# A two-layer hybrid encoder on one core: rope transfers as a task of their own, other planner delays, the fourth head's inputs at another place, decays from still masks in fp32r

## The chip, the core and the metric

The kernel runs on one core of a Trainium2 chip. Its time is the device time of one execution in microseconds, given as the median of three runs. The engines are TensorE (PE: matmuls; PEld: its weight loads), VectorE (DVE), ScalarE (ACT), GpSimd (POOL) and SyncE (SP), which here only issues DMAs. Matmul results go to PSUM accumulators; everything else lies in SBUF.

## The reference

512 tokens (two groups of 256) pass two layers. Each layer has three branches, which share one input projection, and then a convolutional feed-forward part:

```
h = rmsnorm(x) * (1 + sc1) + sh1
p = h @ w_in                                  # one projection, columns split
o_mla = latent attention (low-rank kv, 8 heads, rotary part of width 32)
o_rg  = bidirectional RG-LRU scan
o_gdn = gdn(q, k, v, g_f, beta_f) + flip(gdn(flip(q, k, v, g_b, beta_b)))
m = sum_b sigmoid(gate_b) * (o_b @ w_branch[b]);  x = x + gt1 * (m @ w_out)
x = x + gt2 * ConvGLU(rmsnorm(x) * (1 + sc2) + sh2)
```

`gdn`, the gated delta rule, works in chunks of 64 tokens for each of four heads. The parts that the change touches:

```
g      = cumsum(g within the chunk)
decay  = exp(g_i - g_j)  for j <= i, else 0
A      = strict lower part of (beta k k^T) * decay
Tinv   = (I + A)^-1                           # triangular, per chunk
u, w   = Tinv @ (v beta),  Tinv @ (k beta exp(g))
attn   = (q k^T) * decay;  q_dec = q exp(g);  k_dec = k exp(g_last - g)
per chunk:  v_new = u - w @ state;  o = q_dec @ state + attn @ v_new
            state = state * exp(g_last) + k_dec^T @ v_new
```

## The kernel before

Activations lie with channels on the 128 partitions and the 512 tokens along the free axis. A weight matrix is read in pieces of 128x1024 (tile `raw`, four buffers, issued by SP at L378). ACT rounds each piece to fp32r (`wh`, L391) and DVE takes the rest (`wl`, L298, the helper `sub`). Activations are split in the same way (`hh`, `hl`), and a product is three fp32r matmuls of 128x512 (`mm3`, recorded at L220 like every matmul, since all pass the class `Tensor`).

**The order.** The queues of TensorE and SP follow the order in which the program emits their instructions; those of DVE, ACT and POOL are put in order by a scheduler. The program emits with a planner of its own. The string `BRANCHES` (L33) lists the jobs of a layer's branches: `in6` the first projections; `uq.j`, `uk.j` the queries and keys of attention; `gq.h`, `gk.h`, `gv.h` a GDN head's inputs; `x`, `g`, `b` those of the RG-LRU; `z` the output gate of GDN; `gate.b.d` and `br.b.d` the gate and the projection of branch b; `close` and `mid` sums. Jobs are emitted in that order as fast as a counted clock (`Driver.now`, in planner us, raised by each matmul) goes on. Beside them run generators, the tasks: each emits some instructions and then yields a number from `SLACK` (L61), the planner us after which it goes on. A number so says how much matmul work of the jobs is emitted between one step of a task and the next. `drv.until(event)` holds the jobs until an event's time: the clock jumps from one task's due time to the next, and those tasks' steps are emitted there.

**Rope.** `query(j)` (from L793) computes the attention queries; for j = 5 DVE has the rotated halves ready, and SP sends them to DRAM and back into `Qt` (`drope`, L812; `Qt`, L814):

```
dr = dp.tile([P, 2, T], F32, name="drope", tag="drope")
nc.sync.dma_start(dr, x)
for e in range(2):
    nc.sync.dma_start(Qt[64 + 16 * e:80 + 16 * e], dr.rearrange(...)[e])
ev_q.set(SLACK["rope"])
```

The three DMAs are emitted at once, and the attention's first step waits on `ev_q`.

**Decays.** `solve(h)` (from L1339) handles a GDN head, both directions d and four pairs of chunks t. DVE multiplies the strict mask by the column of g (`gw`, L1355: 128x512 for a direction); TensorE multiplies each 128x128 block of it by the mask `inc` (`gdn_z`, four fp32 matmuls for a direction), and ACT takes the exponential (`E`). A third `gw` (L1373, two halves of 128x256, g against ones) makes `gdn_eg`, from which ACT and DVE make `qd`, the decayed q. `gw` has two buffers, `E` four.

**The inverse.** `gdn_gram`, in two groups, multiplies k by k and by q; DVE forms `B` from it. SP sends the diagonal blocks (`cb`, L1408) to DRAM and back as `Lb`; POOL substitutes in 15 steps (`xt`, `X`, L292 and L298); SP sends the result to DRAM (`dx`, L1440, eight DMAs) and back as `W` (L1444 and L1445, four DMAs). Then `combine` (from L1452) multiplies `W` and `B` on TensorE (`gdn_l16`, `gdn_l32`, `gdn_l64`; a view that joins them prints `gdn_l`). The delays between these steps are `ws`, `z`, `gw`, `eg`, `gram`, `cb`, `dl`, `X`, `dx`, `W`. A head's scan follows: `gdn_rec` (the state), `gdn_o` (the output), and for its norm `ssq` and `spread`.

The constants (masks, identity, ones, selectors) lie in one fp32 tile `cs`, read by one DMA at the start.

Of the kernel before, what the change touches and what calls it, by code (L numbers as in the profile page):

```python
# [8 lines left out]
F32 = mybir.dt.float32  # L9
F32R = mybir.dt.float32r  # L10
# [3 lines left out]
ALU = mybir.AluOpType  # L14
# [4 lines left out]
P = 128  # L19
T = 512  # L20
S = 256
# [15 lines left out]
    g.2 x.3 b.2.0 gate.1.2 b.2.1 gq.2 gk.2 gv.2 gate.1.3 g.3 b.3.0 gate.1.4 b.3.1 gate.1.5 gate.1.6  # L37
    br.1.0 br.1.1 gq.3 br.1.2 z.0 gk.3 br.1.3 gate.2.0 gv.3 gate.2.1 br.1.4 z.1 gate.2.2 br.1.5
    gate.1.7 z.2 br.1.6 gate.2.3 gate.2.4 br.1.7 gate.2.5 z.3 gate.2.6 mid gate.2.7 br.2.0 br.2.1
    br.2.2 br.2.3 br.2.4 br.2.5 br.2.6 br.2.7"""  # L40


def jobs():
# [17 lines left out]
SLACK = {  # L61
    "modev": 0.7, "att_s": 3.2, "att_t": 1.8, "att_e": 1.0, "low_rank": 11.8, "low_rank_out": 152.5, "mla": 0.2,
# [172 lines left out]
def _body(es, tc, nc, xT, cT, wall, wmod, pvec, fng, cst, rope, xinit, yT, dbg):  # L235
    V, A, G = nc.vector, nc.scalar, nc.gpsimd
    drv = Driver()
    PE = Tensor(nc.tensor, drv)
    depth = pvec.shape[1]

    cp = es.enter_context(tc.tile_pool(name="const", bufs=1))
    sp = es.enter_context(tc.tile_pool(name="small", bufs=1))
# [5 lines left out]
    dp = es.enter_context(tc.tile_pool(name="dr", bufs=2, space=DRAM))  # L248
# [19 lines left out]
    ident, ones = C("ident"), C("ones")  # L268
# [4 lines left out]
    dx = [[dp.tile([8, P, 32], F32, name=f"dx{i}{j}", tag=f"dx{i}{j}", bufs=1) for j in range(2)] for i in range(2)]  # L273
# [391 lines left out]
    for k in range(8):  # L665
        t = xp.tile([P, T], F32, name="x", tag="x")
# [8 lines left out]
    for k in range(8):  # L675
        t = stp.tile([P, T], F32, name="sq", tag="t", bufs=4)
# [11 lines left out]
    r = aux_tile(name="spread")  # L688
# [19 lines left out]
    for l in range(depth):  # L708
# [84 lines left out]
        def query(j):  # L793
            if j == 0:
                drv.until(ev_cq)
            ps = gemm(cq)
            if j < 4:
                A.activation(Qt[0:64, 2 * j, :], ps[0:64], AF.Copy, scale=96.0 ** -0.5)
                A.activation(Qt[0:64, 2 * j + 1, :], ps[64:128], AF.Copy, scale=96.0 ** -0.5)
                return  # L800
            cosq, sinq = rep2(rt_[:, 0, :]), rep2(rt_[:, 1, :])
            if j == 4:
                lr["rope"] = mp.tile([P, 4, T], F32, name="rope", tag="Vt")
            ab = lr["rope"][:, 2 * j - 8:2 * j - 6, :]
# [12 lines left out]
        def values():
            Vt = lr["Vt"] = mp.tile([P, 4, T], F32, name="Vt", tag="Vt")
# [250 lines left out]
        for job in JOBS:  # L1069
# [92 lines left out]
            elif k == "out":  # L1162
                d, g = ix
# [23 lines left out]
            elif k == "down":  # L1187
                d, g = ix
# [7 lines left out]
                t = x1[d]  # L1196
# [10 lines left out]
                if (d, g) == (7, 0):  # L1207
                    h = {}
# [16 lines left out]
class GDN:  # L1225
# [16 lines left out]
    def gates(self, ab):  # L1242
        V, A, G, PE = self.V, self.A, self.G, self.PE
        sp, C = self.sp, self.C
# [4 lines left out]
        al = sp.tile([P, 4, 8], F32, name="al_", tag="al_")  # L1249
# [89 lines left out]
    def solve(self, h):  # L1339
# [395 lines left out]
```

## Time and profile before

| | |
|---|---|
| median of three runs | 2016.12 us (2014.07 to 2019.35) |
| the profiled execution | 2019.3 us |
| its span in the trace | 2017.5 us |
| mean granted TensorE clock | 0.986 of full speed |
| PE / DVE / ACT / POOL busy | 1949.8 / 1235.5 / 823.9 / 258.0 us |
| PE instructions; bytes moved by DMA | 11563; 231.44 MB |

An engine's waits are printed as what the idle time before an instruction ended with, in total, number and longest. The timeline gives each record's start and duration; matmul records overlap, so the time that one costs is read from the start of the next. The granted clock (PEclk) is 1 for full speed. Line L220 stands for every matmul, so the tiles' names tell them apart.

### The profile page before, as it was taken

What the parts mean: (1) busy time and instruction counts of PE and PEld (TensorE: products, weight loads), DVE (VectorE), ACT (ScalarE), POOL (GpSimd) and SP (SyncE); (2) the same over time, 40 slices, a digit from 0 to 9 for tenths busy, and PEclk for the clock granted to TensorE, in tenths of its full rate; (3) what the DMA queues carried; (4) which work ended last, traced back from release to release, by engine and by line L of the source; (5) the groups of instructions that cost most, each with busy time, mean ns of one, the idle gap of its engine ahead of it and who ended that gap; (6) DMA issues with size and microseconds to landing.
All of it is one profiled execution on the core that took longest, in us unless ns stands there. A gap on an engine that the chain in (4) does not pass through costs nothing.

```text
span 2017.5 us, 29521 instructions
## 1 busy us (share of the span) xinstructions
PE 1949.8 (97%) x11563; PEld 1564.2 (78%) x11563; DVE 1235.5 (61%) x2324; ACT 823.9 (41%) x1275; POOL 258.0 (13%) x511
## 2 busy tenths in 40 slices
PE   9999999989999999999999999999898999999998
PEld 5777777768777888887877777777687888888887
DVE  5765776755456766652357758776553677676534
ACT  3444366523323544432234534655222344444322
POOL 1100162132200100000011004513130010000000
PEclk9999999999999999999999999999999999999999
DMA  8131443443325233353533123443432533333233
GB/s 318 63 115 53 111 129 113 122 129 94 92 97 186 95 94 104 95 178 106 192 121 94 63 74 113 120 141 110 124 76 74 214 100 94 96 96 100 94 97 102
DMA packets 141851, 231.44 MB, mean 115 GB/s; under 512 B 79760, under 2 KB 84240, under 8 KB 141712
## 3 DMA queue, kind: packets, MB, share of 16 engines
q1 hardware_dynamic: 136240, 221.95, 35.4%
q10 hardware_dynamic: 5472, 7.61, 1.1%
q8 instruction: 91, 1.49, 0.3%
q14 instruction: 48, 0.39, 0.1%
HBM read 221.66 MB, written 7.86 MB: 114 GB/s over the span
## 4 chain that ended last, share of the span: by engine, by line
PE 82%; DVE 5%; POOL 4%; DMA 4%; issue 2%; ACT 2%; SPq 2%; POOLq 0%; ACTq 0%; DVEq 0%
PE mm_up L220 24%; PE mm_down L220 12%; PE mm_gate L220 10%; PE mm_br L220 6%; PE mm_in L220 3%; PE mm_out L220 3%; PE mm_gk L220 2%; PE mod L220 2%; PE mm_gq L220 2%; POOL xt L292 2%; PE mm_gv L220 2%; POOL X L298 2%; PE att_s L220 1%; PE gdn_rec L220 1%; PE gdn_l L220 1%
## 5 line engine op out<-in xcount | busy, mean ns | idle before, releaser
L298 DVE TENSOR_TENSOR wl<-raw,wh 128x1024 fp32r<-128x1024 f32 x304 | 374.0, 1232 | 322.2 <-ACT wh L391 321.6
L391 ACT CAST wh<-raw 128x1024 fp32r<-128x1024 f32 x304 | 318.3, 1049 | 485.3 <-PE mm_down L220 127.9
L220 PE MATMUL mm_up<-hh,wh 128*128 128x512 f32 x704 | 275.8, 392 | 3.4 <-POOL hh L308 3.4
L220 PE MATMUL mm_up<-hl,wh 128*128 128x512 f32 x704 | 275.3, 391 | 0.0
L220 PE MATMUL mm_up<-hh,wl 128*128 128x512 f32 x704 | 275.1, 391 | 0.0
L301 DVE SCALAR_TENSOR_TENSOR cv<-mm_up,pv,cv 128x510 f32<-128x510 f32 x176 | 131.2, 748 | 61.3 <-ACT cv L571 58.0
L220 PE MATMUL mm_gate<-hh,wh 128*128 128x512 f32 x384 | 163.8, 427 | 0.3
L220 PEld LDWEIGHTS mm_up<-hh,wh 128*128 128x128 f32 x704 | 133.0, 189 | 31.6 <-POOL hh L308 3.9
L220 PEld LDWEIGHTS mm_up<-hl,wh 128*128 128x128 f32 x704 | 133.0, 189 | 28.0 <-DVE hl L298 0.3
L220 PEld LDWEIGHTS mm_up<-hh,wl 128*128 128x128 f32 x704 | 133.0, 189 | 27.6
L220 PE MATMUL mm_gate<-hl,wh 128*128 128x512 f32 x384 | 151.2, 394 | 0.0
L220 PE MATMUL mm_gate<-hh,wl 128*128 128x512 f32 x384 | 151.0, 393 | 0.0
L220 PE MATMUL mm_down<-ah,wh 128*128 128x512 f32 (+1 forms) x396 | 145.9, 369 | 0.0
L220 PE MATMUL mm_down<-ah,wl 128*128 128x512 f32 (+1 forms) x396 | 144.9, 366 | 0.6 <-DVE wl L298 0.6
L220 PE MATMUL mm_down<-al,wh 128*128 128x512 f32 (+1 forms) x396 | 144.7, 365 | 0.0
L308 POOL TENSOR_SCALAR hh<-hn 128x256 fp32r<-128x256 f32 x64 | 34.4, 549 | 663.8 <-ACT hn L588 661.2
L571 ACT ACTIVATE cv<-mm_up,pv 128x512 f32<-128x512 f32 x88 | 68.5, 780 | 88.9 <-PE mm_up L220 88.9
L220 PEld LDWEIGHTS mm_gate<-hh,wh 128*128 128x128 f32 x384 | 73.0, 190 | 22.2 <-issue 7.4
L220 PEld LDWEIGHTS mm_down<-ah,wh 128*128 128x128 f32 x396 | 74.7, 189 | 15.0 <-issue 3.3
L220 PEld LDWEIGHTS mm_gate<-hh,wl 128*128 128x128 f32 x384 | 72.7, 189 | 16.4
L220 PEld LDWEIGHTS mm_down<-ah,wl 128*128 128x128 f32 x396 | 74.7, 189 | 12.9 <-DVE wl L298 0.8
L220 PEld LDWEIGHTS mm_down<-al,wh 128*128 128x128 f32 x396 | 74.7, 189 | 11.9
(386 smaller groups left out, 3836.9 us busy)
## 6 DMA issues: line engine op xcount, KB each, us to landing
raw<-in_wall_dram SPq DMA_DIRECT2D x304, 512.0 KB, 3.6
raw<-in_wmod_dram SPq DMA_DIRECT2D x48, 512.0 KB, 3.6
mraw<-in_wmod_dram SPq DMA_DIRECT2D x16, 512.0 KB, 9.9
oraw<-in_wmod_dram SPq DMA_DIRECT2D x16, 512.0 KB, 6.6
hraw<-in_wmod_dram SPq DMA_DIRECT2D x32, 256.0 KB, 5.4
x<-in_xT_dram SPq DMA_DIRECT2D x8, 256.0 KB, 6.1
W<-dx SPq DMA_DIRECT2D x32, 64.0 KB, 3.0
xr<-in_xT_dram ACTq DMA_DIRECT2D x8, 256.0 KB, 3.7
```

The costliest lines, as they stand in the source:

```text
L220: return self.pe.matmul(out, lhsT, rhs, **kw)
L292: (eng or V).tensor_tensor(out, a, b, ALU.mult)
L298: (eng or V).tensor_tensor(out, a, b, ALU.subtract)
L301: V.scalar_tensor_tensor(out, a, s, b, op0, op1)
L308: G.tensor_scalar(hi, x, 1.0, 0.0, ALU.mult, ALU.add)
L391: A.copy(wh, raw)
L571: A.activation(dst, ps, AF.Identity, bias=bias, scale=w[lo])
```

## The change

Four things are changed. The three rope DMAs move from `query(5)` to a task `place`, with a delay before the first (`rope`, 6.0), one before the other two (`rope_out`, 3.0) and one before the event (`rope_in`, 4.0). In `BRANCHES`, `gq.3 gk.3 gv.3` and `z.0` stand ahead of `br.1`, and the jobs of `gate.1`, `gate.2`, `br.1` and `z` behind them are in another order. Five delays of the inverse differ. The decays are computed with the factors exchanged: the masks stay still as the stationary operand, and the moving one is `inc` scaled by g, in two fp32r parts (`gs[0]` the rounded g, `gs[1]` the rest); `gdn_eg` is summed from the same scaled masks against ones, for each direction. The masks `ones`, `strf` and `strb` are read into a tile of their own and rounded to fp32r by POOL (`mk`).

```diff
-    ... gate.1.2 b.2.1 gq.2 gk.2 gv.2 gate.1.3 g.3 b.3.0 gate.1.4 b.3.1 gate.1.5 gate.1.6
+    ... gate.1.2 b.2.1 gq.2 gk.2 gv.2 gate.1.3 g.3 b.3.0 gate.1.4 b.3.1 gq.3 gk.3 gv.3
...
-    ... "cb": 4.0, "dl": 2.5, "X": 18.0, "dx": 3.0, "W": 3.0, ... "rope": 1.5,
+    ... "cb": 5.0, "dl": 4.0, "X": 17.0, "dx": 5.0, "W": 4.0, ... "rope": 6.0, "rope_out": 3.0, "rope_in": 4.0,
...
-    cs = cp.tile([P, NCC], F32, name="cs")
-    nc.scalar.dma_start(cs, cst)
+    cs = cp.tile([P, NCC - NMASK], F32, name="cs")
+    nc.scalar.dma_start(cs, cst[:, 0:NCC - NMASK])
+    mk = cp.tile([P, NMASK], F32R, name="mk")
...
+    m_raw = stp.tile([P, NMASK], F32, name="m_raw")
+    nc.scalar.dma_start(m_raw, cst[:, NCC - NMASK:])
+    G.tensor_scalar(mk, m_raw, 1.0, 0.0, ALU.mult, ALU.add)
...
-                dr = dp.tile([P, 2, T], F32, name="drope", tag="drope")
-                nc.sync.dma_start(dr, x)
-                for e in range(2):
-                    nc.sync.dma_start(Qt[64 + 16 * e:80 + 16 * e], ...)
-                ev_q.set(SLACK["rope"])
+                def place():
+                    yield SLACK["rope"]
+                    dr = dp.tile([P, 2, T], F32, name="drope", tag="drope")
+                    nc.sync.dma_start(dr, x)
+                    yield SLACK["rope_out"]
+                    for e in range(2):
+                        nc.sync.dma_start(Qt[64 + 16 * e:80 + 16 * e], ...)
+                    ev_q.set(SLACK["rope_in"])
+                drv.spawn(place())
...
+        self.gs = [al.bitcast(F32R), sp.tile([P, 4, 8], F32R, name="g_l", tag="spz")]
+        V.tensor_copy(self.gs[0], self.g)
+        self.sub(self.gs[1], self.g, self.f32(self.gs[0]))
...
-        ws = [scaled(C(strict[d]), gt[:, 4 * d + h, :]) for d in range(2)]
-        yield SLACK["ws"]
         E = []
+        pe = self.aux_tile((P, 4, P), "gdn_eg")
         for d in range(2):
+            ws = []
+            for x in self.gs:
+                w = g2.tile([P, 4, P], F32R, name="gw", tag="gw", bufs=2)
+                V.tensor_tensor(w, C(inc[d]).unsqueeze(1).to_broadcast([P, 4, P]),
+                                self.bc(self.f32(x).rearrange("p t e -> p e t")[:, 4 * d + h, :], P), ALU.mult)
+                ws.append(w)
+            yield SLACK["ws"]
             pz = self.aux_tile((P, 4, P), "gdn_z")
-            for t in range(4):
-                PE.matmul(pz[:, t, :], ws[d][:, t, :], C(inc[d]), start=True, stop=True)
+            for i, w in enumerate(ws):
+                PE.matmul(pz, C(strict[d], F32R), w, start=(i == 0), stop=(i == 1))
+            for i, w in enumerate(ws):
+                PE.matmul(pe[:, 1 - d::2, :], C("ones", F32R), w[:, 1 - d::2, :], start=(i == 0), stop=(i == 1))
             e = g2.tile([P, 4, P], F32, name="E", tag="E", bufs=4)
             A.activation(e, pz, AF.Exp)
             E.append(e)
-            if d == 0:
-                yield SLACK["z"]
-
-        w = g2.tile([P, 4, P], F32, name="gw", tag="gw", bufs=2)
-        for d in range(2):
-            V.tensor_tensor(w[:, 1 - d::2, :], self.ones.unsqueeze(1).to_broadcast([P, 2, P]),
-                            self.bc(gt[:, 4 * d + h, 1 - d::2], P), ALU.mult)
-        yield SLACK["gw"]
-        pe = self.aux_tile((P, 4, P), "gdn_eg")
-        for t in range(4):
-            PE.matmul(pe[:, t, :], w[:, t, :], C(inc[1 - t % 2]), start=True, stop=True)
```

The order of instructions follows, as the built programs have it. On SP, around the rope of layer 1 (`raw<-in_wall_dram` is a weight piece, `raw<-in_wmod_dram` a piece of the modulation weights, `xi` a constant), before:

```order
L378 DMA raw<-in_wall_dram 128x1024 x10
L812 DMA drope<-rope 128x1024
L814 DMA Qt<-drope 16x8x512 x2
L378 DMA raw<-in_wall_dram 128x1024 x16
L1051 DMA raw<-in_wmod_dram 128x1024
L1124 DMA xi<-in_xinit_dram 128x128
```

and now:

```order
L381 DMA raw<-in_wall_dram 128x1024 x10
L821 DMA drope<-rope 128x1024
L824 DMA Qt<-drope 16x8x512 x2
L381 DMA raw<-in_wall_dram 128x1024 x16
L1062 DMA raw<-in_wmod_dram 128x1024
L1135 DMA xi<-in_xinit_dram 128x128
```

The lines have other numbers; the place of the three DMAs in the queue is the same.

On TensorE, the decays of head 0 in layer 1, between the matmuls of `gq.0` (numbers behind `hh` and `hl` are buffers), before:

```order
L220 MATMUL gdn_z<-cs,gw 128x128 x4
L220 MATMUL mm_gq<-hh_492,wh 128x512
L220 MATMUL mm_gq<-hl_493,wh 128x512
L220 MATMUL mm_gq<-hh_492,wl 128x512
L220 MATMUL gdn_z<-cs,gw 128x128 x4
L220 MATMUL mm_gq<-hh_578,wh 128x512
```

and now:

```order
L221 MATMUL mm_gq<-hh_484,wl 128x512
L221 MATMUL gdn_z<-gw,mk 128x512 x2
L221 MATMUL gdn_eg<-gw,mk 128x2x128 x2
L221 MATMUL mm_gq<-hh_496,wh 128x512
L221 MATMUL mm_gq<-hl_497,wh 128x512
```

Four matmuls of 128 columns for a direction have become two of 512, and `gdn_eg`, which stood behind both, goes with each; the second direction follows fifteen matmuls later.

On TensorE, the end of head 3's scan in layer 1 (`zb` is a block of zeros that opens an accumulator), before:

```order
L220 MATMUL mm_gate<-hh_590,wl 128x512
L220 MATMUL gdn_rec<-v_5285,kd 128x128 x4
L220 MATMUL gdn_rec<-Ss,kq 128x128 x4
L220 MATMUL gdn_rec<-r,Y 128x128 x4
L220 LDWEIGHTS zb
L220 MATMUL gdn_o<-zb 128x512
```

and now:

```order
L221 MATMUL gdn_rec<-v_5133,kd 128x128 x4
L221 MATMUL mm_gate<-hh_319,wh 128x512
L221 MATMUL mm_gate<-hl_320,wh 128x512
L221 MATMUL mm_gate<-hh_319,wl 128x512
L221 MATMUL mm_gate<-hh_392,wh 128x512
L221 MATMUL mm_gate<-hl_393,wh 128x512
L221 MATMUL mm_gate<-hh_392,wl 128x512
L221 MATMUL spread<-cs,onx 128x128 x4
L221 MATMUL gdn_rec<-Ss,kq 128x128 x4
```

The steps that followed each other directly have matmuls of `gate` between them; further down, matmuls of `gate` and `z` stand between `gdn_rec`, `gdn_o`, `ssq` and `spread` of this head.

## Rows read from the trace of the kernel before

**Rows 1.** The page's first part: busy time, share of the span, instructions.

```profile
PE 1949.8 (97%) x11563; PEld 1564.2 (78%) x11563; DVE 1235.5 (61%) x2324; ACT 823.9 (41%) x1275; POOL 258.0 (13%) x511
```

**Rows 2.** Waits of PE: engine, line, waited for: us in total, times, longest.

```profile
PE gdn_l L220 <- DMA W<-dx: 15.5, 6, 6.2
PE mm_uk L220 <- ACT wh L391: 9.6, 2, 4.8
PE spread L220 <- DVE onx L301: 4.6, 2, 2.3
PE ssq L220 <- DVE osq L295: 4.0, 2, 2.0
...
PE gdn_rec L220 <- DVE r L295: 2.7, 2, 1.3
...
PE ssq L220 <- DVE acc L295: 1.7, 1, 1.7
PE gdn_rec L220 <- ACT Ss L1544: 1.4, 2, 0.7
```

**Rows 3.** Windows: us, busy PE, PEld, DVE, ACT, POOL (instructions), PEclk, DMA, GB/s.

```profile
117.90:124.70 6.80, 6.38 (x14) 4.61 (x15) 3.17 (x4) 2.34 (x4) 0.00 (x0) 0.50 0.49 153
428.50:435.30 6.80, 4.17 (x72) 3.46 (x73) 1.55 (x2) 0.00 (x0) 0.00 (x0) 0.50 0.84 236
561.60:568.40 6.80, 4.48 (x19) 4.23 (x20) 2.53 (x12) 0.00 (x0) 0.00 (x0) 0.50 0.00 0
1111.20:1114.60 3.40, 3.21 (x8) 2.01 (x8) 2.11 (x2) 0.93 (x2) 0.00 (x0) 0.50 0.34 119
1421.80:1425.20 3.40, 3.11 (x69) 2.69 (x70) 1.56 (x2) 0.00 (x0) 0.00 (x0) 0.50 0.79 297
1554.90:1561.70 6.80, 6.17 (x19) 5.24 (x20) 2.54 (x6) 0.62 (x1) 0.00 (x0) 0.50 0.00 0
```

**Rows 4.** Timeline of PE: start, duration, engine, line, operation, out<-in, shape.

```profile
212.87 0.39 PE L220 MATMUL mm_br<-oh,wl 128*128 128x512 f32 x1
...
223.75 0.39 PE L220 MATMUL mm_gq<-hh,wl 128*128 128x512 f32 x1
223.98 1.05 PE L220 MATMUL gdn_z<-cs,gw 128*128 128x128 f32 x8
224.78 0.48 PE L220 MATMUL mm_gq<-hh,wh 128*128 128x512 f32 x1
225.10 0.40 PE L220 MATMUL mm_gq<-hl,wh 128*128 128x512 f32 x1
```

**Rows 5.** Timeline of PE, matmuls of 256 columns.

```profile
1003.79 0.28 PE L220 MATMUL mm_down<-al,wh 128*128 128x256 f32 x1
1003.91 0.28 PE L220 MATMUL mm_down<-ah,wl 128*128 128x256 f32 x1
```

**Rows 6.** Tile gw in layer 1: count, ns min/median/max, first and last start.

```profile
L1355 DVE TENSOR_TENSOR gw<-cs,g__805 x8: 685/692/727, 221.4 to 386.5; 128x512 f32<-128x512 f32 x8
```

**Rows 7.** Timeline of PE and SP, head 2 of layer 1, gram to inverse.

```profile
391.69 1.02 PE L220 MATMUL gdn_gram<-kq 128*128 128x256 f32 x4
...
426.41 0.38 SPq L1444 DMA_DIRECT2D W<-dx  x1
...
431.13 1.08 PE L220 MATMUL gdn_l<-W,B 32*32 32x32 f32 x64 [6.17 <-DMA W<-dx]
```

**Rows 8.** Timeline of SP's queue around the rope of layer 1.

```profile
78.35 0.33 SPq L378 DMA_DIRECT2D raw<-in_wall_dram  x1
...
105.62 0.37 SPq L378 DMA_DIRECT2D raw<-in_wall_dram  x1
```

**Rows 9.** Waits of SP's queue.

```profile
SPq L1440 <- POOL X L298: 68.5, 8, 13.9
...
SPq L812 <- DVE rope L298: 45.4, 2, 23.4
```

**Rows 10.** Tile xt, both layers.

```profile
L292 POOL TENSOR_TENSOR xt<-Lb,X x120: 211/384/1396, 250.4 to 1504.0; 128x120 f32<-128x120 f32 x8, 128x112 f32<-128x112 f32 x8, 128x104 f32<-128x104 f32 x8, 128x96 f32<-128x96 f32 x8
```

More of the change, by code (lines that the diff above doesn't have):

```diff
@@ L36 @@
     br.0.6 br.0.7 close gq.1 gk.1 gv.1 x.0 x.1 b.0.0 g.0 b.0.1 gate.1.0 g.1 b.1.0 x.2 b.1.1 gate.1.1
-    g.2 x.3 b.2.0 gate.1.2 b.2.1 gq.2 gk.2 gv.2 gate.1.3 g.3 b.3.0 gate.1.4 b.3.1 gate.1.5 gate.1.6
-    br.1.0 br.1.1 gq.3 br.1.2 z.0 gk.3 br.1.3 gate.2.0 gv.3 gate.2.1 br.1.4 z.1 gate.2.2 br.1.5
-    gate.1.7 z.2 br.1.6 gate.2.3 gate.2.4 br.1.7 gate.2.5 z.3 gate.2.6 mid gate.2.7 br.2.0 br.2.1
+    g.2 x.3 b.2.0 gate.1.2 b.2.1 gq.2 gk.2 gv.2 gate.1.3 g.3 b.3.0 gate.1.4 b.3.1 gq.3 gk.3 gv.3
+    gate.1.5 z.0 br.1.0 br.1.1 gate.1.6 br.1.2 br.1.3 gate.1.7 z.1 br.1.4 br.1.5 br.1.6 br.1.7 gate.2.0
+    gate.2.1 z.2 gate.2.2 gate.2.3 gate.2.4 gate.2.5 z.3 gate.2.6 mid gate.2.7 br.2.0 br.2.1
     br.2.2 br.2.3 br.2.4 br.2.5 br.2.6 br.2.7"""
@@ L82 @@
 _n = 0
-for _name, _w in [("ident", 128), ("ones", 128), ("incf", 128), ("incb", 128), ("strf", 128),
-                  ("strb", 128), ("sel1", 2), ("sel2", 4), ("sel4", 8), ("off16", 64)]:
+for _name, _w in [("ident", 128), ("incf", 128), ("incb", 128), ("sel1", 2), ("sel2", 4), ("sel4", 8),
+                  ("off16", 64), ("ones", 128), ("strf", 128), ("strb", 128)]:
     CC[_name] = (_n, _w)
@@ L87 @@
 NCC = _n
+NMASK = 3 * P
 def constants():
@@ L254, in _body, with C @@
     fill(sp, 96)
-    cs = cp.tile([P, NCC], F32, name="cs")
-    nc.scalar.dma_start(cs, cst)
-    def C(name):
+    cs = cp.tile([P, NCC - NMASK], F32, name="cs")
+    nc.scalar.dma_start(cs, cst[:, 0:NCC - NMASK])
+    mk = cp.tile([P, NMASK], F32R, name="mk")
+    def C(name, dtype=F32):
         o, w = CC[name]
-        return cs[:, o:o + w]
+        o -= NCC - NMASK
+        return mk[:, o:o + w].bitcast(dtype) if o >= 0 else cs[:, CC[name][0]:CC[name][0] + w]
     pv = cp.tile([P, depth, NPV], F32, name="pv")
@@ L810, in query @@
                 add(x[:, 1, :], x[:, 1, :], y[:, 0, :])
-                dr = dp.tile([P, 2, T], F32, name="drope", tag="drope")
-                nc.sync.dma_start(dr, x)
-                for e in range(2):
-                    nc.sync.dma_start(Qt[64 + 16 * e:80 + 16 * e], dr.rearrange("(h p) e t -> e p h t", p=16)[e])
-                ev_q.set(SLACK["rope"])
+                def place():
[4 more added lines that the diff above has]
+                    for e in range(2):
+                        nc.sync.dma_start(Qt[64 + 16 * e:80 + 16 * e], dr.rearrange("(h p) e t -> e p h t", p=16)[e])
+                    ev_q.set(SLACK["rope_in"])
+                drv.spawn(place())
         def values():
@@ L1349, in solve @@
         inc, strict = ("incf", "incb"), ("strf", "strb")
-        gt = self.g.rearrange("p t e -> p e t")
-        def scaled(mask, cols):
-            w = g2.tile([P, 4, P], F32, name="gw", tag="gw", bufs=2)
-            V.tensor_tensor(w, mask.unsqueeze(1).to_broadcast([P, 4, P]), self.bc(cols, P), ALU.mult)
-            return w
-        ws = [scaled(C(strict[d]), gt[:, 4 * d + h, :]) for d in range(2)]
-        yield SLACK["ws"]
         E = []
+        pe = self.aux_tile((P, 4, P), "gdn_eg")
         for d in range(2):
+            ws = []
[5 more added lines that the diff above has]
+            yield SLACK["ws"]
             pz = self.aux_tile((P, 4, P), "gdn_z")
-            for t in range(4):
-                PE.matmul(pz[:, t, :], ws[d][:, t, :], C(inc[d]), start=True, stop=True)
+            for i, w in enumerate(ws):
+                PE.matmul(pz, C(strict[d], F32R), w, start=(i == 0), stop=(i == 1))
+            for i, w in enumerate(ws):
+                PE.matmul(pe[:, 1 - d::2, :], C("ones", F32R), w[:, 1 - d::2, :], start=(i == 0), stop=(i == 1))
             e = g2.tile([P, 4, P], F32, name="E", tag="E", bufs=4)
@@ L1367, in solve @@
             E.append(e)
-            if d == 0:
-                yield SLACK["z"]
-        w = g2.tile([P, 4, P], F32, name="gw", tag="gw", bufs=2)
-        for d in range(2):
-            V.tensor_tensor(w[:, 1 - d::2, :], self.ones.unsqueeze(1).to_broadcast([P, 2, P]),
-                            self.bc(gt[:, 4 * d + h, 1 - d::2], P), ALU.mult)
-        yield SLACK["gw"]
-        pe = self.aux_tile((P, 4, P), "gdn_eg")
-        for t in range(4):
-            PE.matmul(pe[:, t, :], w[:, t, :], C(inc[1 - t % 2]), start=True, stop=True)
         qd = g2.tile([P, 4, P], F32, name="qd", tag="qd", bufs=2)
```

4 rows, old and new, of the table SLACK are left out of this document.

## The prediction

> **What bounds the kernel now.** The page's first part comes first: TensorE is busy for 97% of the span [rows 1]. Whatever shortens the time therefore removes TensorE work or one of the 67 us in which it stands still. The waits by engine come second: they say what ends the idle time, and the reader is to see that few causes carry it [rows 2]: 15.5 us behind the DMA that brings `W`, 9.6 us behind the split of late weights in `mm_uk`, and four rows (2.7, 1.4, 4.0, 4.6 us) of head 3's last steps. Third come the windows on the stretches in which the granted clock is 0.5, the lower of its two levels (1.2 instead of 2.4 GHz): each lies on one of those stalls [rows 3]. A stall so costs twice, its idle time and half of the work done in the slow stretch. The program's order, before and now, comes last.
>
> **The decays in fp32r.** Before, each head issues three groups of four 128x128 fp32 matmuls (two `gdn_z`, one `gdn_eg`). One group starts at 223.98 and the next matmul at 224.78, and that one takes 0.32 us to its successor where 0.23 is usual [rows 4]: 0.80 + 0.09 = 0.89 us. 3 x 8 heads in two layers = 24 groups: 21.4 us. Now each head and direction issues two fp32r matmuls of 512 columns (0.227 us apart: 10.88 us for the 48 steps from 212.87 to 223.75 [rows 4]) and two of 256 (0.12 us apart [rows 5]), 0.69 us, no fp32 among them: 16 x 0.69 = 11.1 us. Nothing covers TensorE, so the sum is -10.3 us. A mixed row for 2x128 columns doesn't exist; at 0.227 each it would be -6.9, and no less than the 128-column price bounds it at -11.
>
> DVE makes four 128x512 masks at 0.69 us instead of two and two halves [rows 6]: under 1.4 us more per head, on an engine that is not the bound. The second pair must wait until TensorE has read the first (two buffers) and be ready 3.0 planner us later: 0.69 of matmuls plus 1.4 of DVE leave some 1 us for other DVE work ahead. I take 2 us for all heads; bounds 0 and 16 (1 us at each of 16 pairs, the size of the shorter waits in [rows 2]).
>
> **Head 3's inputs earlier.** Before, at the end of each layer's branches the three `gdn_rec` steps, `gdn_o`, `ssq` and `spread` follow each other with no other matmul between. Now six `gate` matmuls and a `spread` stand between the second and the third, then 15, 24, 12 and 36 of `gate` and `z`. At 0.227 us these are 1.4 and more, 3.4, 5.4, 2.7 and 8.2 us; the single waits there are 0.7, 1.3, none, 2.0 and 2.3 us [rows 2], so every one is covered. Idle time saved: 2.7 + 1.4 + 4.0 + 4.6 = 12.7 us in both layers. The slow stretches there start at 561.6 and 1554.9; TensorE works 4.48 and 6.17 us in them [rows 3], half of which is lost: 5.3 us. Sum -18.0; I take -17, as a shorter wait may stay, with bounds -10 and -18. The moved jobs' own matmuls are the same number. `br.1` starts later than before, so its wait for the scans has more cover, not less.
>
> **The other delays: W.** The 15.5 us are six waits, heads 0, 2 and 3 in either layer; the longest, 6.2 us, is head 2's. For it the second gram group starts at 391.69, and `gdn_l` starts at 431.13, when `W` is there, after 6.17 us in which TensorE has nothing else [rows 7]: 39.4 us are needed where 33.3 were given. Counted in the built order, 156 instead of 120 512-column matmuls stand between the two: 36 x 0.227 = 8.2 us, and with two transposes and one decay group about 9.6: 42.9 us are given, 3.5 to spare. Head 0 gets 27 more, 6.1 us, less 1.3 for cheaper decays, against a share of the small rest. Head 3 waits for head 2's release anyway. Against that, SP now issues the last step only after one more weight load for the modulation: before, one `raw` stood between the eight `dx` and the four `W` issues, now a `raw` of each kind does, and such a load can itself wait for its buffer. From `W`'s first issue at 426.41 to 431.13 it took 4.7 us [rows 7], more than the 4.0 planner us that the last delay gives, so wherever SP is held some 1 us stays. I keep 1 us for each of four heads. The clock's share was (4.17 + 3.11) / 2 = 3.6 us [rows 3]. Sum: -15.5 - 3.6 + 4 = -15; bounds -19 and -5.
>
> TensorE's clock rows bear on these two parts. The Trainium skill ("TensorE: Matmul & The Clock Gate", Terms) prices a slow stretch at its whole length times the missing share of pulses. By it the four stretches, 23.8 us, would be 11.9 us, and the sum 3 us larger. The rows show idle time inside them, which I have counted already, so I charge only the busy part, 9.0 us.
>
> **The rope transfers.** SP issues its last weight load before `drope` at 78.35 and the next only at 105.62 [rows 8]; between them it stands at `drope` until DVE is done with `rope`, 23.4 us the longer of two such waits [rows 9]. This makes the first of the two stalls of 4.8 us in `mm_uk` [rows 2]. The new task issues the same three DMAs after 6.0 and 3.0 planner us. But uk.0 waits on the planner's clock for the low-rank result (a delay of 152.5), and the clock runs through the task's delays there before any further weight load is emitted. In the built order the three DMAs stand between the same loads as before, in both layers, and `att_s` follows the same matmuls. I cost it at 0, bounds -1 and +1: what hides a gain is that SP is still held by the same wait.
>
> **Start and gates.** The masks come by a third DMA on ACT's queue and one POOL pass. The first user, `ssq`, waits 1.7 us for `acc` anyway [rows 2]: 0, bounds 0 and +1. Two more 128x32 DVE operations in `gates` lie inside a planned delay of 13.7: 0. The other waits, not touched, stay.
>
> **Sum.** -10.3 + 2 - 17 - 15 = -40.3 us. The profiled execution took 2019.3 us (span 2017.5); it gives 1979.0. The median of the runs shown is 2016.1, 3.2 us lower, which gives 1975.8. I forecast 1978, between the two.
>
> **Rivals.**
> - *The W wait stays* (0.17). For it: the extra load ahead of `W`, and POOL's chain before it. One `xt` step (they shrink from 120 to 8 elements) takes 384 ns at the median and 1396 at most [rows 10], so something stretches single steps by up to 1 us, and 3.5 us of reserve are a few of these. If two thirds of 15.5 + 3.6 stay, 12.7 us, 4 of which are in the sum, the time is 1987; if all stays, 1993. The Trainium skill ("SBUF — State Buffer", SBUF: two separate sides) speaks for this rival: a DVE operation with two SBUF inputs and a GpSimd one lock each other out for a whole instruction, and the new masks are four of that sort. The spread of `xt` agrees. By it the added masks, under 1.4 us a head, could hold the chain back by as much, within the reserve, so it adds to the chance and not to the price.
> - *New waits at the decays* (0.12). The second pair of masks is late behind other DVE work, or the accumulator for `gdn_eg`, now held from the start of both directions, is missing to someone. 1 us at each of 16 pairs and half as much again for slow stretches: +22, 2000. Against: no wait of `gdn_z` or `gdn_eg` for DVE among the rows of before.
> - *The rope does come free* (0.03): 9.6 us idle and (6.38 + 3.21) / 2 = 4.8 of slow clock [rows 3] go too: 1978 - 14 = 1964. The order speaks against it.
> - *Slower* (0.04): SP, one queue in order, reaches `dx` after 17 instead of 18 planner us and stands there until POOL has finished `X`; the weight loads behind it come late, and TensorE starves as in `mm_uk`. SP already stands at `dx` for 68.5 us in eight waits, 13.9 the longest [rows 9]. A starved step costs what `mm_uk` does, 4.8 + 2.4 = 7.2 us; from six of the eight heads on the gain of 40 is gone, and all eight make 1978 + 58 = 2036. Against: before, these eight waits cost TensorE nothing that [rows 2] shows.
> - The change may pay as stated (0.64): 1968 to 1988, its own range.
>
> **How the numbers follow.** About 0.3%, 6 us, is what a measurement of this kernel can tell from no change. The forecast, the rope rival and the first two rivals are all faster than 2010; some of the weight of the last but one and of mixtures of them falls within 2010 to 2022: faster 0.93, same 0.03, slower 0.04. The range holds the forecast's own range, the rope case and the W case, and nearly reaches the decay case: 1964 to 1998.
>
> **What would show it.** Decays: `gdn_z` with 32 and `gdn_eg` with 32 matmul rows, about 0.7 us from a group's start to the next matmul. Tail: no idle rows at `ssq`, `spread` and `gdn_rec` beyond 1 us in all, and no stretch of clock 0.5 there. W: the row below 5 us, no single wait above 2. Rope: `mm_uk` again with two stalls of about 4.8 us, which is the test of my reading of the order; if they are gone, that step is wrong. Any row of more than 3 us on `gdn_z`, `mm_gate` or `mm_gk` behind `wl` or `wh` would speak for the last two rivals.

## The result and the profile after

The changed kernel takes 1970.0 us (median of four runs, 1969.0 to 1971.4), the kernel before, in four runs, 2017.7: a ratio of 0.976 (95% interval 0.974 to 0.979), 47.7 us less. The forecast was 1978 us with a range of 1964 to 1998. The profiled execution took 1969.0 us with a span of 1966.9, 50.6 us under the span before.

The page's first part and then the waits of PE in the changed kernel, to be read against [rows 1, 2] (all matmuls now have line L221):

```profile
PE 1928.6 (98%) x11435; PEld 1547.0 (79%) x11435; DVE 1238.5 (63%) x2328; ACT 822.5 (42%) x1275; POOL 255.5 (13%) x512
```

```profile
PE mm_uk L221 <- ACT wh L394: 9.6, 2, 4.8
...
PE gdn_tr L225 <- DVE kq L304: 2.2, 4, 0.8
...
PE mm_gv L221 <- DVE wl L301: 1.7, 2, 0.9
PE gdn_l L221 <- DMA W<-dx: 1.3, 1, 1.3
...
PE mm_b L221 <- DVE wl L301: 1.0, 1, 1.0
...
PE ssq L221 <- DVE osq L298: 0.4, 2, 0.2
```

TensorE stays the bound and stands still for 38.3 us (1966.9 - 1928.6) instead of 67.7 (2017.5 - 1949.8). The wait for `W` is down from 15.5 to 1.3 us, the four rows of head 3's last steps from 12.7 to nothing (the 0.4 at `ssq` are two waits of 0.2 at 373 and 1342 us, in another head's steps), and `mm_uk` has its 9.6 us as before. `mm_b` is new and `gdn_tr` larger, 2.7 us more together. The trace has two records for an fp32 matmul of 128 columns: the 96 of the old decays were 192 records, the 64 new matmuls are 64, which makes the 128 instructions fewer.

The timeline of PE at the first decays, against [rows 4]:

```profile
219.61 0.62 PE L221 MATMUL gdn_z<-gw,mk 128*128 128x512 f32 x2
220.07 0.39 PE L221 MATMUL gdn_eg<-gw,mk 128*128 128x256 f32 x2
220.30 0.40 PE L221 MATMUL mm_gq<-hh,wh 128*128 128x512 f32 x1
220.53 0.40 PE L221 MATMUL mm_gq<-hl,wh 128*128 128x512 f32 x1
```

A direction costs 220.30 - 219.61 = 0.69 us, and the matmul behind it runs at its usual 0.23. The same head 2 as in [rows 7], PE and SP:

```profile
381.78 1.02 PE L221 MATMUL gdn_gram<-kq 128*128 128x256 f32 x4
...
416.24 0.38 SPq L1450 DMA_DIRECT2D W<-dx  x1
...
425.29 0.75 PE L221 MATMUL gdn_l<-W,B 32*32 32x32 f32 x64
```

From the second gram group to `gdn_l` 43.5 us pass (425.29 - 381.78; 42.9 were forecast), all but 0.3 of them other work, and no wait for `W` ends there. SP around the rope, against [rows 8]:

```profile
73.57 2.96 SPq L381 DMA_DIRECT2D raw<-in_wall_dram  x2
98.64 0.33 SPq L821 DMA_DIRECT2D drope<-rope  x1
101.22 0.81 SPq L824 DMA_DIRECT2D Qt<-drope  x2
102.12 1.80 SPq L381 DMA_DIRECT2D raw<-in_wall_dram  x4
```

The hold is there as before: the last load goes out at about 76, the next at 102.12, and then four at once.

### The profile page after: what moved, and what is told of

Same layout as the page of the kernel before. It is cut to its first block, busy times and chain, and to the rows that moved or that the text cites. A ratio compares the mean times of both kernels' runs of the same rounds, so it can differ in the third digit from the quotient of the medians.

```text
span 1966.9 us, 29250 instructions
## 1 busy us (share of the span) xinstructions
PE 1928.6 (98%) x11435; PEld 1547.0 (79%) x11435; DVE 1238.5 (63%) x2328; ACT 822.5 (42%) x1275; POOL 255.5 (13%) x512
## 4 chain that ended last, share of the span: by engine, by line
PE 89%; DVE 4%; DMA 2%; ACT 1%; issue 1%; POOL 1%; SPq 0%; DVEq 0%; POOLq 0%; ACTq 0%
PE mm_up L221 25%; PE mm_gate L221 13%; PE mm_down L221 12%; PE mm_br L221 7%; PE mm_in L221 4%; PE mm_out L221 3%; PE mod L221 2%; PE mm_z L221 2%; PE mm_gq L221 2%; PE mm_x L221 2%; PE mm_gv L221 2%; PE mm_g L221 2%; PE att_s L221 2%; PE gdn_rec L221 1%; PE gdn_l L221 1%
## 5 line engine op out<-in xcount | busy, mean ns | idle before, releaser
L221 PE MATMUL mm_up<-hh,wh 128*128 128x512 f32 x704 | 276.7, 393 | 3.5 <-POOL hh L311 3.5
L221 PE MATMUL mm_up<-hl,wh 128*128 128x512 f32 x704 | 276.3, 392 | 0.0
L221 PE MATMUL mm_up<-hh,wl 128*128 128x512 f32 x704 | 275.9, 392 | 0.0
L221 PE MATMUL mm_gate<-hh,wh 128*128 128x512 f32 x384 | 160.6, 418 | 0.0
L221 PEld LDWEIGHTS mm_up<-hh,wh 128*128 128x128 f32 x704 | 133.5, 190 | 31.8 <-POOL hh L311 3.9
L221 PEld LDWEIGHTS mm_up<-hl,wh 128*128 128x128 f32 x704 | 133.5, 190 | 28.2 <-DVE hl L301 0.3
L221 PEld LDWEIGHTS mm_up<-hh,wl 128*128 128x128 f32 x704 | 133.6, 190 | 27.7
L221 PE MATMUL mm_gate<-hh,wl 128*128 128x512 f32 x384 | 150.2, 391 | 0.0
L221 PE MATMUL mm_gate<-hl,wh 128*128 128x512 f32 x384 | 150.1, 391 | 0.0
L221 PE MATMUL mm_down<-ah,wh 128*128 128x512 f32 (+1 forms) x396 | 146.0, 369 | 0.0
L221 PE MATMUL mm_down<-ah,wl 128*128 128x512 f32 (+1 forms) x396 | 144.9, 366 | 0.6 <-DVE wl L301 0.6
L221 PE MATMUL mm_down<-al,wh 128*128 128x512 f32 (+1 forms) x396 | 144.8, 366 | 0.0
L221 PEld LDWEIGHTS mm_down<-ah,wh 128*128 128x128 f32 x396 | 74.7, 189 | 15.0 <-issue 3.3
L221 PEld LDWEIGHTS mm_gate<-hh,wh 128*128 128x128 f32 x384 | 72.2, 188 | 18.0 <-issue 4.9
L221 PEld LDWEIGHTS mm_down<-ah,wl 128*128 128x128 f32 x396 | 74.7, 189 | 12.9 <-DVE wl L301 0.8
L221 PEld LDWEIGHTS mm_gate<-hh,wl 128*128 128x128 f32 x384 | 72.1, 188 | 16.0
L221 PEld LDWEIGHTS mm_down<-al,wh 128*128 128x128 f32 x396 | 74.7, 189 | 11.8
```

The costliest lines, as they stand in the source:

```text
L221: return self.pe.matmul(out, lhsT, rhs, **kw)
```

## The experiments

Each ratio is to runs of the kernel before taken together with that row's, whose medians are 2018.7 to 2020.3 us; 0.001 is 2 us.

| run | what | median us | ratio (95%) |
|---|---|---|---|
| e1 | changed, rope later | 1957.6 | 0.969 (0.968 to 0.971) |
| e2 | changed, five delays back | 1986.4 | 0.984 (0.983 to 0.986) |
| e3 | changed, jobs back | 1994.0 | 0.988 (0.987 to 0.990) |
| e4 | changed, decays back | 1977.2 | 0.980 (0.978 to 0.981) |
| e5 | changed, three delays back | 1981.0 | 0.981 (0.980 to 0.983) |
| e6 | changed, two delays back | 1971.8 | 0.977 (0.976 to 0.979) |
| e7 | e2, dx issued by POOL | 1977.6 | 0.980 (0.978 to 0.981) |
| e8 | changed, rope back | 1970.0 | 0.976 (0.975 to 0.978) |
| e9 | e1 with filler matmuls | 1954.6 | 0.966 (0.965 to 0.968) |
| e10 | before, delays alone | 2006.8 | 0.993 (0.991 to 0.995) |
| e11 | before, jobs alone | 1993.7 | 0.986 (0.985 to 0.988) |
| e12 | before, decays alone | 2031.8 | 1.005 (1.003 to 1.007) |

### The rope: e1 and e8

```diff
 def place():
+    yield ev_ckv            # e1: wait for the low-rank result's event first
     yield SLACK["rope"]
```

```diff
-    drv.spawn(place())      # e8: all three DMAs at once, as before
+    nc.sync.dma_start(dr, x); ...; ev_q.set(1.5)
```

> The changed kernel with one line more in the rope task: it first waits for the planner's event of the low-rank result, then for its delay of 6.0. In the built order TensorE's queue is unchanged row for row; on SP two more weight loads stand ahead of drope in either layer (12 instead of 10). Theory (the stalls of 4.8 us in mm_uk come from weight loads held on SP behind drope, and the new task did not lift that): the two stalls go, 9.6 us, and with them the half of TensorE's work in the two stretches at clock 0.5 that begin at 112.3 and 1085.1 in the changed kernel, about 2 us each: 1970 - 9.6 - 4 = 1956 us, no mm_uk row above 0.5 us. Rival (the stall is the transfer time of the weights themselves or the wait for split buffers): the stalls stay, 1970 us. Second rival (the rope result now reaches attention late): a wait of att_s for Qt of several us takes the stall's place, 1965 to 1972 us.

> The changed kernel with the rope transfers issued at once as before, in no task. The built orders of TensorE and SP are those of the changed kernel row for row. Theory (the task as such does nothing, since the three DMAs stand behind the same loads): 1970 us, within 2 us, with both stalls of 4.8 us in mm_uk. Rival (the scheduler of DVE and ACT places the rope work better with the task): 1973 us or more.

e8 takes 1970.0 us like the changed kernel, with both stalls of 4.8: the task as such does nothing. e1 takes 1957.6, 12.4 less. Its SP timeline:

```profile
75.86 15.65 SPq L381 DMA_DIRECT2D raw<-in_wall_dram  x4
100.93 0.33 SPq L822 DMA_DIRECT2D drope<-rope  x1
```

Four loads instead of two leave ahead of `drope`; its waits of PE have no row of `mm_uk`, and a small new one:

```profile
PE mm_uv L221 <- ACT Vt L849: 1.3, 2, 0.7
```

With TensorE's order untouched, two weight loads moved ahead of one held DMA are worth 12 us. So the forecast's reading of the order was right, and the change left this gain on the table.

### What the five delays do: e2, e5, e6 and e7

```diff
-"cb": 5.0, "dl": 4.0, "X": 17.0, "dx": 5.0, "W": 4.0     # changed kernel
+"cb": 4.0, "dl": 2.5, "X": 18.0, "dx": 3.0, "W": 3.0     # e2
+"cb": 4.0, "dl": 2.5, "X": 18.0, "dx": 5.0, "W": 4.0     # e5
+"cb": 5.0, "dl": 4.0, "X": 17.0, "dx": 3.0, "W": 3.0     # e6
```

> The changed kernel with the five old delays of the inverse (cb 4.0, dl 2.5, X 18.0, dx 3.0, W 3.0). Theory (the W term is made by how much matmul work lies between a head's second gram group and its first use of W, and the moved inputs and the new decays lengthen that too): the built order gives 132 instead of 156 matmuls of 512 columns for head 2, 126 instead of 147 for head 0, 111 instead of 135 for head 3; before they were 120, 120 and 147 with waits of 6.2, 1.1 and 0.7. Waits on W of about 0 to 0.5, 1.7 and 1.0 us come back in either layer, 6 us in all, and up to 3 us of slow clock: 1976 to 1979 us. Rival (the delays alone carry the W term): the whole 14 us of waits and 3.6 of slow clock come back, 1988 us.

e2 came out at 1986.4, outside the theory's 1976 to 1979 and near the rival's 1988, but not by the rival's way. Waits of PE in e2:

```profile
PE mod L221 <- DMA raw<-in_wmod_dram: 8.1, 2, 4.7
...
PE gdn_l L221 <- DMA W<-dx: 2.3, 3, 1.7
```

`W` waits only 1.0 us more than in the changed kernel. What is new is `mod`, the modulation's matmul, in front of which TensorE waits for a weight load. SP, and then PE, of e2 at that place:

```profile
290.32 0.33 SPq L381 DMA_DIRECT2D raw<-in_wall_dram  x1
305.74 1.81 SPq L1446 DMA_DIRECT2D dx<-X  x4
307.64 3.27 SPq L1446 DMA_DIRECT2D dx<-XT  x4
311.01 0.43 SPq L1062 DMA_DIRECT2D raw<-in_wmod_dram  x1
```

```profile
314.97 1.08 PE L221 MATMUL mod<-raw,csil 128*32 128x256 f32 x8 [4.71 <-DMA raw<-in_wmod_dram]
```

and SP of the changed kernel there:

```profile
295.03 0.33 SPq L1062 DMA_DIRECT2D raw<-in_wmod_dram  x1
307.61 1.81 SPq L1446 DMA_DIRECT2D dx<-X  x4
```

In e2 SP issues nothing from 290.65 to 305.74, since it stands at head 1's `dx` until POOL has made `X`, and the modulation's load stands behind it. Of SP's waits in e2:

```profile
SPq L1446 <- POOL X L301: 47.5, 8, 15.0
```

In the changed kernel the same hold (to 307.61) ends in no wait of `mod` for a load, because this load has left at 295.03. Three runs tested that:

> The changed kernel with the three old delays ahead of dx (cb 4.0, dl 2.5, X 18.0) and the new ones behind it (dx 5.0, W 4.0). With all five old delays, mod waited 4.7 and 3.3 us for a modulation weight load that stood on SP behind the dx of head 1, and SP stood at dx for POOL's X. In the built order of this kernel that load stands behind dx as there (in the changed kernel it stands ahead of it), while head 2 has 150 matmuls of 512 columns between gram and W. Theory (the delays ahead of dx decide, by the place of that load on SP): the waits of mod come back, 8 us and some 3 us of slow clock, no waits for W: 1980 to 1985 us. Rival (the delays behind dx decide, by the distance to W): 1970 to 1972 us.

> The changed kernel with the two old delays behind dx alone (dx 3.0, W 3.0). The load of the modulation stands ahead of head 1's dx as in the changed kernel; the distances from gram to W are 138 matmuls for heads 0 and 2, 117 for head 3, some 3 us shorter. Theory of the place on SP: no wait of mod; the distances still cover W but for head 3 or 0, under 1 us in either layer: 1970 to 1973 us. Rival of the distance: W waits and slow clock back, 1980 us or more.

```diff
-nc.sync.dma_start(v[...], b[32 * o:32 * o + 32])      # e7: dx, on the kernel of e2
+nc.gpsimd.dma_start(v[...], b[32 * o:32 * o + 32])
```

> The kernel of e2 (all five old delays, 1986 us there) with the eight dx transfers of a head issued by POOL, which makes X and XT, instead of SP. TensorE's order is that of e2 row for row; on SP only dx is gone. Theory (mod waits because SP stands at dx until POOL has finished X): the waits of mod of 4.7 and 3.3 us go, with their slow clock: 1972 to 1977 us, unless POOL's issues take long enough to delay W, which then shows as a wait of gdn_l. Rival (the load is late because its raw buffer is late or the transfers are crowded): mod waits on, 1984 us or more.

e5 takes 1981.0: the delays ahead of `dx` alone bring the wait back. e6 takes 1971.8, the same as the changed kernel within the intervals, though its `W` waits are 2.9 us where under 1 in either layer was expected. Waits of PE, first of e5, then of e6:

```profile
PE mod L221 <- DMA raw<-in_wmod_dram: 11.4, 2, 5.7
```

```profile
PE gdn_l L221 <- DMA W<-dx: 2.9, 2, 2.1
```

e7, with the order of e2 on TensorE, takes 1977.6, 8.8 less than e2; SP no longer meets `dx`, and POOL issues it:

```profile
295.06 0.33 SPq L381 DMA_DIRECT2D raw<-in_wall_dram  x1
300.95 0.33 SPq L1062 DMA_DIRECT2D raw<-in_wmod_dram  x1
```

The load leaves at 300.95 and no wait of `mod` for a load is left. The cause of that wait is shown: what the delays ahead of `dx` buy is the place of one load on SP. It isn't the whole of e2's 16.4 us: e7 came out just above its 1972 to 1977 and stays 7.6 us behind the changed kernel. Its waits of `mm_b`, `gdn_rec`, `ssq` and others are longer by a few us in all, and no run took that rest apart.

### The jobs and the decays, undone: e3 and e4

e3 is the changed kernel with `BRANCHES` of before, e4 with the masks, `gates` and `solve` of before:

```diff
-gate.1.4 b.3.1 gq.3 gk.3 gv.3 gate.1.5 z.0 br.1.0 ...        # changed kernel
+gate.1.4 b.3.1 gate.1.5 gate.1.6 br.1.0 br.1.1 gq.3 ...      # e3
```

```diff
-    PE.matmul(pz, C(strict[d], F32R), w, ...)                 # changed kernel
+    PE.matmul(pz[:, t, :], ws[d][:, t, :], C(inc[d]), ...)    # e4, for four t
```

> The changed kernel with the old order of jobs (the fourth head's inputs and z behind br.1 as before). Theory: the waits of head 3's last steps come back, 12.3 us, with 5.3 us of slow clock; the order gives head 2 only 141 matmuls of 512 columns between gram and W, 1.4 us too few, in either layer, 3 us: 1970 + 20 = 1990 us, with ssq and spread waiting 2.0 and 2.3 us again. Rival (the head's steps have enough cover by the other changes, since they start earlier): under 5 us come back, 1975 us or less.

> The changed kernel with the old decays (fp32 masks as the moving side scaled, three groups of four 128x128 matmuls, one constants tile, three waits of the planner). Theory: each layer's decays cost 10.2 instead of 5.9 us of TensorE, 8.6 us in both, and the start loses up to 2 us; W and the tail stay covered (144, 153 and 138 matmuls for heads 0, 2 and 3): 1979 to 1981 us. Rival (the new decays' gain is half eaten by DVE's extra masks, so undoing them costs little): 1974 us or less. Second rival (the fp32 transitions cost more than the groups show): 1984 us or more.

e3 takes 1994.0, 4 us above the theory, and e4 1977.2, 2 us below its range; both lie nearer to it than to the rivals. Waits of PE in e3:

```profile
PE gdn_l L221 <- DMA W<-dx: 6.2, 4, 3.0
PE spread L221 <- DVE onx L304: 4.6, 2, 2.3
PE ssq L221 <- DVE osq L298: 4.4, 4, 2.0
...
PE gdn_rec L221 <- DVE r L298: 2.7, 2, 1.3
```

The tail's waits are back within a tenth (0.4 of the `ssq` row is the other head's), two more rows of `gdn_rec` add 2.5 us there, and `W` waits more than forecast (6.2, which is 4.9 more than in the changed kernel, where 3 were forecast). In e4, `gdn_z` and `gdn_eg` of a layer take 10.1 us of TensorE, summed from each start to the next, against 5.9 in the changed kernel.

### Each part alone: e10, e11 and e12

These put the five new delays, the new `BRANCHES`, or the new decays alone into the kernel before.

> The kernel before with the five new delays alone. In the built order head 2 has 144 instead of 120 matmuls of 512 columns between gram and W, head 0 144 instead of 120, head 3 165 instead of 147, and the load of the modulation stands ahead of head 1's dx. Theory: of the 15.5 us of waits for W about 1 us stays, and the 3.6 us of slow clock go: 2018.7 - 18 = 2001 us; the tail waits stay at 12.7 us. Rival (the longer delays only move the stall to mod or to the tail): 2010 us or more.

> The kernel before with the new order of jobs alone. Theory: the tail's waits of 12.7 us and 5.3 us of slow clock go; the distances from gram to W are 120, 129 and 111 matmuls for heads 0, 2 and 3 instead of 120, 120 and 147, so the W waits go from 15.5 to about 10 us: 2018.7 - 18 - 6 = 1995 us, with up to 4 us less if the slow clock behind W goes too. With e10 and the decays (7 us by e4) the three parts then add up to the whole change, 48 us. Rival (the parts overlap: without the new delays the moved inputs only make head 3 wait for W): 2003 us or more.

> The kernel before with the new decays alone (and the masks in their own tile). Theory (TensorE's work is what counts: 10.2 us of gdn_z and gdn_eg in a layer become 5.9): 8.6 us less, and the shorter run of steps gives head 0 126 instead of 120 matmuls between gram and W, so its waits of 1.1 and 1.2 us go: 2019 - 8.6 - 2 = 2008 us, 2006 to 2011; head 2's waits of 6.2 and 5.5 us and the tail stay. Rival (undone in the changed kernel, the decays cost 7 us, so some of their gain is given back): 2012 us. Rival on the other side (the masks' second pair waits for its buffers where the order is tighter): waits of gdn_z or gdn_eg for gw appear and the time is 2016 us or more.

e11 came as expected in its time, with `W` waits of 5.8 us where about 10 were forecast. e10 missed its 2001 by 6 us and lies nearer to its rival's 2010. Waits of PE in e10, then two windows of it at clock 0.5 (columns as in [rows 3]):

```profile
PE gdn_l L220 <- DMA W<-dx: 2.9, 2, 2.1
```

```profile
540.60:550.80 10.20, 8.19 (x36) 7.48 (x36) 2.14 (x4) 0.59 (x1) 0.00 (x0) 0.50 0.01 2
1530.40:1540.60 10.20, 8.19 (x37) 7.48 (x36) 2.14 (x4) 0.59 (x1) 0.00 (x0) 0.50 0.00 0
```

Most of the `W` waits go (2.9 us stay where about 1 was forecast), but the tail, where two more rows of `gdn_rec` wait 2.5 us, now holds more slow work: with two shorter stretches there (3.30 and 4.49 us of work) half of 24.2, 12.1 us, against 5.3 before. That is the part of the rival that speaks of the tail. e12 refutes its theory: the decays alone make the kernel slower, 2031.8 us. Its waits:

```profile
PE gdn_l L221 <- DMA W<-dx: 17.9, 5, 4.8
...
PE mod L221 <- DMA raw<-in_wmod_dram: 7.0, 2, 4.0
```

No row names `gdn_z` or `gdn_eg`, so it isn't the rival of the masks. Instead what follows has shifted against the old delays: the modulation's load falls behind head 1's `dx`, as in e2 (it leaves at 310.46 us, `dx` from 305.42; before, it left at 297.97 and `dx` from 310.43), and `W` waits 2.4 us more. Nine windows at clock 0.5 lie on these stalls and the tail's, with 43.0 us of TensorE's work, where the four of before hold 17.9 [rows 3]: half of the difference, 12.6 us, is lost on top. 7.0 + 2.4 + 12.6 - 8.6 = +13.4 us; the spans differ by +12.8. The sum leaves out the slow stretches at other places, the start and small waits; these come to about -1 us together, and that they nearly cancel is chance. The first and the last of the nine:

```profile
314.00:320.80 6.80, 6.26 (x20) 4.38 (x21) 0.00 (x0) 0.00 (x0) 0.00 (x0) 0.50 0.96 293
...
1570.10:1573.50 3.40, 3.02 (x11) 2.85 (x12) 1.10 (x4) 0.00 (x0) 0.00 (x0) 0.50 0.00 0
```

By the medians the three alone make -13.5, -26.7 and +11.5 us, -28.7 together; the whole change makes -47.7. Some 19 us come only from having them together.

### The cost of a slow stretch: e9

```diff
     drv.drain_spare()
+    keep_warm(1.6)          # seven matmuls on zeros, at three places
```

> The kernel of e1 (rope transfers later, 1957.6 us there) with seven matmuls on zeros, 1.6 us, put into TensorE's queue at each of the three places between the last norm and the first matmul of the feed-forward part or of the second layer, where TensorE waits 1.76, 1.63 and 1.76 us for hh. The wait itself stays, only filled. Theory (a stall costs twice, and the second part, half of TensorE's work in the stretch at clock 0.5 behind it, is 5.81, 3.40 and 5.36 us over two there): the three stretches at clock 0.5 go, 7.3 us: 1950 us. Rival (the 0.7 us of idle for modev ahead of it, or something else, sets the clock): 1957 us, stretches as before. Second rival (the filler runs longer than the wait): 1958 us or more.

Windows on the stretches at clock 0.5 around those places, of e1 and then of e9:

```profile
616.50:623.30 6.80, 5.81 (x14) 4.48 (x15) 5.26 (x15) 3.81 (x7) 2.75 (x6) 0.50 0.00 0
998.80:1002.20 3.40, 3.40 (x8) 2.65 (x9) 2.89 (x8) 2.13 (x4) 1.94 (x4) 0.50 0.00 0
1579.00:1585.80 6.80, 5.36 (x13) 4.12 (x14) 5.71 (x16) 3.51 (x7) 2.75 (x6) 0.50 0.00 0
```

```profile
615.10:618.50 3.40, 3.40 (x11) 1.63 (x10) 2.93 (x10) 2.08 (x4) 1.77 (x4) 0.51 0.00 0
994.00:1000.80 6.80, 6.80 (x22) 4.61 (x23) 4.58 (x17) 2.93 (x6) 2.36 (x5) 0.50 0.06 22
1577.70:1581.10 3.40, 3.40 (x11) 1.78 (x12) 2.62 (x10) 1.77 (x4) 1.00 (x2) 0.50 0.00 0
```

The stretches stay, shorter at two places and longer at one, so filling the wait for `hh` does not hold the clock at 1.00; they now begin 0.4 to 1.4 us behind the 0.7 us wait for `modev` ahead of it. That fits the first rival, but no run fills this wait too, so it isn't shown that it is the cause. 1954.6 us is 3 us below e1, but the intervals of the two touch: whether the filler gains anything is not settled. Both e1 and e9 beat the changed kernel.

## Why the prediction came out

The direction, the range and most steps held; the sum was 7 us too small against the medians (40.3 against 47.7). The terms against the two profiled executions (decays summed from each start to the next; slow clock as half of TensorE's work in the stretches):

| step | forecast | measured |
|---|---|---|
| decays, TensorE's work | -10.3 | -9.9 (-8.6: 10.2 to 5.9 a layer; -1.3 at the matmuls behind them) |
| wait for the second pair of masks | +2 | 0 |
| head 3's last steps, idle and clock | -17 | -18.0 (-12.7 and -5.3) |
| W, idle and clock | -15 | -17.8 (-14.2 and -3.6) |
| rope | 0 | waits 0 (e8); clock -1.3 (9.59 us of work in the slow stretches, now 6.97) |
| start | 0 | -2.1 |
| other waits (`mm_x`, `mm_gv`, `mm_gq`, `gdn_l` for issue, less `gdn_tr`, `mm_b`, `ssq`) | none | -1.7 |
| slow clock at the norms, between the waits for `modev` and `hh` | none | +3.7 |

The table explains 47.1 of the 50.6 us in the spans; the rest is not traced. The mis-sized terms are the two reserves: +2 us at the masks and 4 us of leftover `W` waits, of which 0 and 1.3 came. The last four rows, which the forecast put at nothing or did not have, nearly cancel (-1.4 us), which is luck. The reserve that the forecast gave head 2 was right (43.5 us given against 42.9).

The last row corrects a reading. The prediction says of the stretches at clock 0.5 that each lies on one of the stalls that it names. This holds for the six of [rows 3]; there are others, at the start, at the end and at the norms. These are the three places of e9 in the kernel before, then in the changed one:

```profile
650.40:653.80 3.40, 3.04 (x7) 2.39 (x8) 2.73 (x8) 2.20 (x5) 2.25 (x5) 0.50 0.00 0
1030.00:1034.00 4.00, 3.16 (x13) 2.39 (x14) 3.33 (x9) 2.80 (x6) 2.35 (x5) 1.00 0.00 0
1640.20:1647.00 6.80, 5.13 (x14) 3.80 (x13) 6.13 (x19) 3.27 (x6) 2.75 (x6) 0.50 0.00 0
```

```profile
620.90:627.70 6.80, 6.01 (x14) 4.68 (x15) 5.06 (x14) 3.81 (x7) 2.75 (x6) 0.50 0.00 0
1003.20:1006.60 3.40, 3.40 (x8) 2.65 (x9) 2.89 (x8) 2.13 (x4) 1.94 (x4) 0.50 0.00 0
1590.30:1597.10 6.80, 6.15 (x14) 4.76 (x15) 4.93 (x14) 3.80 (x8) 2.76 (x6) 0.50 0.00 0
```

TensorE's waits ahead are nearly the same in both (0.70 to 0.73 us for `modev`, then 1.64 to 1.77 for `hh`), yet 8.17 us of its work fell into slow stretches before and 15.56 now, and in the second place the clock stayed at 1.00 before. So the same stall does not always cost the same: its idle time is sure, the slow stretch behind it is not.

The Trainium skill ("SBUF — State Buffer", SBUF: two separate sides) made me raise the chance of the first rival: DVE's masks and POOL's steps would lock each other out. The tile `xt` in the changed kernel, against [rows 10]:

```profile
L295 POOL TENSOR_TENSOR xt<-Lb,X x120: 210/424/1361, 245.8 to 1429.4; 128x120 f32<-128x120 f32 x8, 128x112 f32<-128x112 f32 x8, 128x104 f32<-128x104 f32 x8, 128x96 f32<-128x96 f32 x8
```

The median grew by 40 ns and the longest didn't, but the sum stayed: the 120 steps take 59.4 us in either trace, and the eight heads' chains, each from its first `xt` to its last, 128.9 us before and 129.0 now. Of the steps that take over 0.15 us more than the shortest of their shape, 30 before and 38 now, 26 and 28 overlap a tensor_tensor of DVE. So the trace fits the lock, but the added masks cost the chain nothing that can be measured here, and `W` came in time.

The decays' term was read from one group; over a layer a new group takes 0.74 us (5.9 / 8), not 0.69. The loss at the matmul behind a group is there as forecast, but not behind each: before, 16 of the 24 take 0.31 to 0.32 us to their successor, and now none of the 16 takes more than 0.24, some 1.3 us in all.

Two steps named the wrong carrier though their sums were right.

- *The other delays: W.* The prediction credited the five delays with the distance from gram to `W`. The new jobs alone cut these waits to 5.8 us (e11) and the delays alone to 2.9 (e10), so with the new jobs and decays in place the delays are hardly needed for it (e6: +1.6 us; e2: +1.0). What they are needed for is `mod` (e5, e7).
- *Slower (0.04).* The mechanism of that rival is real, and close by: SP at `dx`, a load behind it, a starved TensorE. It decides e2, e5 and e12. The prediction reckoned with `X` alone, 17 instead of 18; `cb` and `dl` are 1.0 and 1.5 longer, so `dx` comes 1.5 planner us later than with the old delays, and the load slips ahead of it. So the change went the other way than this rival feared.

Adding the parts as if each stood alone was also a flaw that the total didn't show: e12 saves the decays' 8.6 us of work and is slower all the same.

## What to carry to other kernels

Where one engine is the bound, the sum of its removed work, its removed waits and half of its work in the slow stretches behind them gave the gain within a few us here; but a slow stretch behind the same wait came and went between kernels, so leave some us of range for it. The two reserves for feared leftovers would have served better in the range than in the sum. When a DMA in an in-order queue waits for a slow producer, look up which load stands right behind it and who needs that next: one load ahead of or behind `dx` is worth 9 to 11 us here (e7 against e2, e5), two loads ahead of `drope` 12. Delays tuned for one shape of work did not fit another (e12): test a part alone and in company before you credit it.

## What was not expected of the hardware

- The slow stretch at the start (14 to 19 us, clock 0.50) comes in some profiled executions and not in others of the same code: `mm_in` begins at 23.12 us in the changed kernel and at 25.37 in e1, whose TensorE instructions are the same in the same order. The wait of `ssq` ahead of it is 0.59 us in the one and 1.71 in the other. About 2 us of the 50.6 in the spans are this chance.
- Eight `dx` transfers took POOL from 310.23 to 315.99 us to issue in e7, 5.8 us with a memset of 0.33 among them. On SP they took from 305.74 to 310.91 in e2, 5.2 us, and 3.9 in the changed kernel (307.61 to 311.51).
